# Two chunks of an input projection at a time by seven half products

## The chip, the cores and the metric

The kernel runs on one core of a Trainium2 chip: TensorE (PE) multiplies matrices, VectorE (DVE), ScalarE (ACT) and GpSimd (POOL) work elementwise, and SyncE (SP) issues most transfers. The metric is the device time of one execution in microseconds; less is better.

## The reference, cut to what matters

One inference step of a hybrid encoder with two layers. 512 prompt rows and 128 sample rows (8 sequences of 16) share all weights, so a layer works on 640 rows of 1024 features. A layer starts with one wide projection, whose columns feed four branches and their gates:

```python
(a_u, a_v, a_g, b_x, b_g, c_q, c_kv, c_kr, c_g, m_q, gate_logits) = split_cols(x @ w_in)
oa, v_rows = gmlp_branch(a_u, a_v, ...);      oa = oa * silu(a_g)
ob, conv_new, h_new = rglru_branch(b_x, ...); ob = ob * silu(b_g)
oc, ckv_new, kr_new = mla_branch(c_q, c_kv, c_kr, ...); oc = oc * silu(c_g)
om = mem_attend(m_q, mem_k, mem_v)
g = sigmoid(gate_logits)                      # 4 x 1024 columns
merged = g[0] * (oa @ w_br[A]) + g[1] * (ob @ w_br[B]) + g[2] * (oc @ w_br[C]) + g[3] * (om @ w_br[M])
x_new = layer_norm(ALPHA * x + merged @ w_out, ln_g, ln_b)
```

Everything is fp32. The branches are a chunked spatial gating (A), a short convolution with a linear recurrence (B), a latent attention (C) and an attention to a memory (M).

## The kernel before, in words

Every large product is done in three passes of a faster matmul type: a float32 matrix is split into a rounded part (`wh`, `xh`, type fp32r) and the rest (`wl`, `xl`), and `wh*xh + wh*xl + wl*xh` is accumulated in PSUM. `split` (L143 to L146) makes the two parts: a cast on ACT, a subtraction on DVE.

The activations are kept by features: `xh` and `xl` are two tiles each of 128 partitions x 4 x 640. Of the projection, 54 chunks of 128 columns per layer go through `fm_chunk`: it loads 128 x 1024 weights (`wload`, 512 KB), splits them, and calls `fm_product` (L112 to L126), which issues 8 x 3 steps of two matmuls of 320 columns each, 48 in all, into the two banks of one `acc` tile in PSUM (tag "acc", two tiles, four banks).

Chunks by use, per layer: 4 for `gelu_u` (u of A), 4 for the gate of C, 4 for the gate of A (`sga`), 2 for the memory's query (`mq`), 4 for the gate of B, 4 for the recurrence's input (`lru_in`), and 32 for the merge gates. `merge` is a generator: one step computes a gate chunk f of branch bi, its branch product y from `bhl` (the split branch result) and `w_br`, and adds the gated product to `macc` (on POOL for bi 1 and 2, on DVE in the last). In the last merge the sum is split again (`mgh`, `mgl`) for the output projection (L953).

The order of a layer in the program: latents and v, `gelu_u`, the queries (`q_ps`), the gate of C, keys and values, the latent attention of the sample (8 steps b: `ss_ps`, softmax `p_s`, transposes, `pt_s`, `olat_ps`), that of the prompt (4 blocks of 128 rows x 4 pairs of heads: `sc_ps`, maximum `mx`, exponential `p_c`, transposes `pt_ps`, copies `pt_c`, `pv_ps`), the gate of A, the mix of A (L623), the queries to the memory, the gate of B, the memory attention of the sample, then recurrence, memory attention of the prompt (`mem_prompt`) and first merge interleaved by hand, three more merges, output projection and normalisation.

The order on each engine is set at compile time by a list scheduler: an instruction is placed when its inputs are ready and its engine is free, earlier in the program first. Tiles live in pools; tiles of one tag share a number of slots. Those that matter here: tag "t" (five slots: `p_s`, `pt_s`, `olat`, `p_c`, `pt_c`, `p_m`, ...), tag "f" (two slots: `sga`, `mixb`, `g`, `a2`), "x" (four slots of 10 KB per partition) and "o" (four of 10 KB: `ep`, `v`, `oc`, `oa`, `um`, `ob`, `mgh`, `mgl`), "s" (one of 20 KB: `sc`, `wmx`, `bhl`, `wos`), "raw" (three of 4 KB) and "wh" and "wl" (two each, and two small ones).

The functions that the change touches, with their line numbers:

Of the kernel before, what the change touches and what calls it, by code (L numbers as in the profile page):

```python
# [9 lines left out]
F32 = mybir.dt.float32  # L10
# [30 lines left out]
def encoder_step(  # L41
# [19 lines left out]
    def xtile(name):  # L61
        return xp_.tile([128, 4, T], F32R, tag="x", name=name)
# [6 lines left out]

    def stile(shape, dtype, name):  # L70
        return big.tile(shape, dtype, tag="s", name=name)
# [31 lines left out]
    def wraw(src, n=1024):  # L103
        raw = wp.tile([128, n], F32, tag="raw", name="raw", bufs=3)
        nc.sync.dma_start(out=raw, in_=src)
        return raw

    def wload(src, n=1024):
        raw = wraw(src, n)
        sz = "" if n > 512 else "2"  # L110
        h = wp.tile([128, n], F32R, tag="wh" + sz, name="wh")
        lo = wp.tile([128, n], F32R, tag="wl" + sz, name="wl")  # L112
        split(h, lo, raw)
        return h, lo

# [12 lines left out]
    def tm_products(outs_, lhs_h, lhs_l, nc_, nk_per, width, load):  # L128
        for ci in range(nc_):
# [3 lines left out]
            for n, (j, a, w) in enumerate(steps):  # L133
                for t, o in enumerate(outs_):
# [3 lines left out]
                        rhs=w[:, j * width:(j + 1) * width],  # L138
# [36 lines left out]
    xscr = dr.tile([T, D], F32, name="xscr")  # L175

    for l in range(L):
# [12 lines left out]
        mh = kvtile([128, KD, 256], F32R, "mem_h")  # L190
        ml = kvtile([128, KD, 256], F32R, "mem_l")
        def mem_in(k):
            mt = wraw(ins["memT"][:, k:k + 4, :].rearrange("p a b -> p (a b)"))
            for m in range(2):
                split(
                    mh[:, k + 2 * m:k + 2 * m + 2, :], ml[:, k + 2 * m:k + 2 * m + 2, :],
                    mt[:, m * 512:(m + 1) * 512].rearrange("p (a b) -> p a b", a=2),
                )

        def w_mem(c):  # L200
            r = wload(ins["w_mem"][l, c])
# [42 lines left out]
        def w_c(c):  # L244
            if l > 0:
                return wload(ins["w_c"][l, c], 832)
            if c > 0:
                r = wload(ins["w_c"][l, c], 832)
                x_in(2 * c, 2)
                return r  # L250
            raw = wp.tile([128, 832], F32, tag="raw", name="raw", bufs=3)
            h = wp.tile([128, 832], F32R, tag="wh", name="wh")
            lo = wp.tile([128, 832], F32R, tag="wl", name="wl")
            for j in range(2):
                js = slice(416 * j, 416 * j + 416)
                nc.sync.dma_start(out=raw[:, js], in_=ins["w_c"][l, c][:, js])
                x_in(j, 1)
                split(h[:, js], lo[:, js], raw[:, js])
            return h, lo
# [7 lines left out]
        def fm_chunk(c, l=l):  # L267
            h, lo = wload(ins["w_fm"][l, c])
            o = acc("fm")
            fm_product(  # L270
                o,
                lambda k: h[:, k * 128:(k + 1) * 128],
                lambda k: lo[:, k * 128:(k + 1) * 128],
                xhk, xlk, KD,
            )
            return o[:, :, 0:TH]

# [29 lines left out]
        def w_v(c):  # L307
            r = wload(ins["w_v"][l, c])
# [799 lines left out]
```

## Time and profile before

| what | value |
|---|---|
| runs shown (3) | 1448.62 us median, 1448.54 to 1449.63 |
| profiled execution: span from first to last instruction | 1446.2 us |
| PE busy | 1426.0 us (99%), 9376 matmuls |
| DVE, ACT, POOL busy | 709.0 us (49%), 530.9 us (37%), 138.7 us (10%) |
| DMA | 134 MB, 28% of the 16 engines' time |

The time of the profiled execution itself is its span plus what lies around it, which the trace doesn't show; the median of the runs is 2.4 us above the span. A matmul's busy time overlaps that of the next, so its pace is read from the chain, not from its mean.

### The profile page before, as it was taken

How to read it: one execution, taken by the hardware profiler on the slowest of the kernel's cores; microseconds unless marked ns; L12 is line 12 of the kernel's file. 1: busy time of each engine (PE TensorE's matmuls, PEld its weight loads, DVE VectorE, ACT ScalarE, POOL GpSimd, SP SyncE). 2: the span in 40 equal slices, each digit the busy share in tenths (PEclk: the TensorE clock that was granted, in tenths of full speed). 3: DMA queues.
4: the chain of work that ended last, by engine and by line, in shares of the span. 5: the costliest groups of instructions: out<-in, count | busy, mean ns of one | idle time of the engine just before them, and what ended most of it. 6: DMA issues, size and time to landing. Idle time of an engine off the chain costs nothing.

```text
span 1446.2 us, 22712 instructions
## 1 busy us (share of the span) xinstructions
PE 1426.0 (99%) x9376; PEld 1322.8 (91%) x9376; DVE 709.0 (49%) x1264; ACT 530.9 (37%) x931; POOL 138.7 (10%) x200
## 2 busy tenths in 40 slices
PE   8999999999999999999999999999999999999997
PEld 8899888989999999998898998788899999999986
DVE  5643577386542232444834535763954322323546
ACT  5533443265532232333234434432664222222320
POOL 2020000010101112100111100000111011211000
PEclk9999999999999999999999999999999999999999
DMA  8342113213222222134372222032132222222323
GB/s 288 115 142 74 52 36 111 78 59 111 74 80 73 81 73 77 61 101 156 115 229 92 85 73 66 30 117 81 48 121 69 73 81 73 81 64 73 114 73 110
DMA packets 51065, 134.16 MB, mean 93 GB/s; under 512 B 5777, under 2 KB 14897, under 8 KB 49937
## 3 DMA queue, kind: packets, MB, share of 16 engines
q1 hardware_dynamic: 49328, 127.54, 27.7%
q0 software_dynamic: 1632, 5.16, 1.0%
q8 instruction: 74, 1.21, 0.4%
q14 instruction: 31, 0.25, 0.1%
HBM read 123.59 MB, written 7.78 MB: 91 GB/s over the span
## 4 chain that ended last, share of the span: by engine, by line
PE 93%; DVE 4%; ACT 1%; DMA 1%; issue 1%; DVEq 0%; POOL 0%; SPq 0%; ACTq 0%
PE fm L120 52%; PE y L120 14%; PE y_ps L953 6%; PE v L135 4%; PE c L135 3%; PE sc_ps L568 3%; PE pv_ps L592 2%; PE mem L135 2%; PE q_ps L120 1%; PE pt_ps L585 1%; PE gate L773 1%; PE mix L623 1%; PE ss_ps L513 1%; DVE wl L146 1%; PE ptm_ps L831 1%
## 5 line engine op out<-in xcount | busy, mean ns | idle before, releaser
L146 DVE TENSOR_TENSOR wl<-raw,wh 128x1024 fp32r<-128x1024 f32 (+4 forms) x203 | 206.0, 1016 | 419.4 <-issue 288.8
L120 PE MATMUL fm<-xh,wh 128*128 128x320 f32 x1728 | 406.9, 313 | 0.0
L120 PE MATMUL fm<-xl,wh 128*128 128x320 f32 x1728 | 404.1, 312 | 0.0
L145 ACT CAST wh<-raw 128x1024 fp32r<-128x1024 f32 (+4 forms) x203 | 179.2, 883 | 477.6 <-PE fm L120 326.8
L120 PEld LDWEIGHTS fm<-xh,wh 128*128 128x128 f32 x1728 | 289.3, 188 | 8.3 <-issue 5.0
L120 PEld LDWEIGHTS fm<-xl,wh 128*128 128x128 f32 x1728 | 289.6, 188 | 5.6 <-issue 4.9
L120 PE MATMUL fm<-xh,wl 128*128 128x320 f32 x1728 | 281.0, 311 | 0.0
L120 PEld LDWEIGHTS fm<-xh,wl 128*128 128x128 f32 x1728 | 258.7, 188 | 3.4 <-issue 2.6
L120 PE MATMUL y<-bhl,wh 128*128 128x320 f32 x896 | 141.6, 309 | 0.0
L120 PEld LDWEIGHTS y<-bhl,wh 128*128 128x128 f32 x896 | 133.6, 188 | 0.0
L884 POOL TENSOR_TENSOR macc<-macc,g 128x640 f32<-128x640 f32 x32 | 62.1, 1941 | 340.5 <-DVE g L881 340.5
L881 DVE SCALAR_TENSOR_TENSOR g<-g,y 128x640 f32<-128x640 f32 x48 | 39.4, 821 | 95.8 <-PE y L120 95.8
L120 PE MATMUL y<-bhl,wl 128*128 128x320 f32 x448 | 76.6, 309 | 0.0
L865 ACT ACTIVATE g<-fm 128x640 f32<-128x640 f32 x64 | 45.2, 706 | 81.4 <-PE fm L120 81.3
L120 PEld LDWEIGHTS y<-bhl,wl 128*128 128x128 f32 x448 | 68.3, 188 | 0.0
L568 PE MATMUL sc_ps<-kT,qT 128*128 128x128 f32 (+7 forms) x128 | 45.6, 450 | 0.0
L577 ACT ACTIVATE p_c<-sc_ps,mx 128x128 f32<-128x128 f32 (+3 forms) x64 | 33.6, 532 | 4.5 <-DVE mx L574 4.5
L953 PE MATMUL y_ps<-wo,mgh 128*128 128x512 f32 x120 | 35.1, 396 | 0.0
L587 ACT COPY pt_c<-pt_ps 128x128 f32<-128x128 f32 (+3 forms) x32 | 13.6, 425 | 52.8 <-PE pt_ps L585 52.8
L574 DVE TENSOR_REDUCE mx<-sc_ps 128x1 f32<-128x128 f32 (+3 forms) x64 | 30.3, 477 | 0.5
L585 PE MATMUL pt_ps<-ident,p_c 128*128 128x128 f32 x160 | 28.4, 275 | 1.7 <-DVE pt_c L587 1.7
L585 PEld LDWEIGHTS pt_ps<-ident,p_c 128*128 128x128 f32 x160 | 19.9, 140 | 10.8 <-issue 4.3
(295 smaller groups left out, 1675.2 us busy)
## 6 DMA issues: line engine op xcount, KB each, us to landing
raw<-in_w_fm SPq DMA_DIRECT2D x108, 512.0 KB, 3.5
raw<-in_w_br SPq DMA_DIRECT2D x48, 256.0 KB, 2.6
mcache<-in_mem_kv SPq DMA_DIRECT2D x8, 1024.0 KB, 4.8
raw<-in_w_out SPq DMA_DIRECT2D x16, 512.0 KB, 4.3
raw<-in_w_v SPq DMA_DIRECT2D x8, 512.0 KB, 4.0
raw<-in_w_mem SPq DMA_DIRECT2D x8, 512.0 KB, 3.5
raw<-in_w_c SPq DMA_DIRECT2D x7, 416.0 KB, 5.1
xr<-in_x SPq DMA_DIRECT2D x10, 256.0 KB, 3.0
```

Of the source, the lines that this page charges most:

```text
L120: PE.matmul(out=out[:, j, 0:TH], lhsT=a(k), rhs=b(k)[:, j * TH:(j + 1) * TH], start=(n == 0), stop=(n == len(steps) - 1),)
L135: PE.matmul(out=o[:, 0:width], lhsT=a(ci * nk_per + j)[:, t * 128:(t + 1) * 128], rhs=w[:, j * width:(j + 1) * width], start=(ci == 0 and ...
L145: ACT.copy(out=dst_h, in_=src)
L146: DVE.tensor_tensor(out=dst_l, in0=src, in1=dst_h.bitcast(F32), op=ALU.subtract)
L568: PE.matmul(out=s[:, 0:nk], lhsT=qT[0:kr_, h, ts_], rhs=kT[h // 4][0:kr_, h % 4, 0:nk], start=True, stop=True,)
L574: DVE.tensor_reduce(out=mx, in_=s[:, 0:nk], axis=AX.X, op=ALU.max, negate=True)
L577: ACT.activation(out=p[:, 0:nk], in_=s[:, 0:nk], func=AF.Exp, bias=mx, accum_out=sm)
L585: PE.transpose(tps[:, k * 128:(k + 1) * 128], p[:, k * 128:(k + 1) * 128], ident)
L865: ACT.activation(out=halves(g), in_=o, func=AF.Tanh, scale=0.5)
L881: DVE.scalar_tensor_tensor(out=halves(g), in0=halves(g), scalar=1.0, in1=y, op0=ALU.add, op1=ALU.mult)
L884: (POOL if bi < 3 else DVE).tensor_tensor(out=m, in0=m, in1=g, op=ALU.add)
L953: PE.matmul(out=o[j], lhsT=a[k // 4][:, k % 4, t * 128:(t + 1) * 128], rhs=w[:, j * 512:(j + 1) * 512], start=(k == 0 and p == 0), stop=(k ...
```

## The change

Two chunks c and c + 1 are computed together by `fm_pair`, with Strassen's scheme in Winograd's form: blocks are the two chunks, the two halves of the 1024 features and the two halves of the 640 rows. Seven products of half the depth and half the rows take the place of eight. Their weight operands are three blocks as loaded (a11, a12, a22) and four sums of blocks, made on POOL; their activation operands are blocks of x and four sums (`xt`), made once per layer by `x_sums`, one of them in place of a block of x. The seven results are combined by DVE from PSUM. 46 of the 54 chunks go this way, in 23 pairs per layer: gates of A and B, `mq`, `lru_in` and all merges. `gelu_u` and the gate of C stay as they were, since they come before `x_sums`.

```diff
-    xp_ = ctx.enter_context(tc.tile_pool(name="xpool", bufs=4))
-    op_ = ctx.enter_context(tc.tile_pool(name="opool", bufs=4))
+    op_ = ctx.enter_context(tc.tile_pool(name="opool", bufs=10))
...
+    def wraw(src, n=512):
+        raw = wtile("raw", n, "raw", 6)
+    def whl(raw, n=512):
+        h, lo = wtile("wh", n, "wh", 4), wtile("wl", n, "wl", 4)
+        split(h, lo, raw)
...
+    def spill(bi, k, src):
+        nc.sync.dma_start(out=oscr[bi][k], in_=src)
...
+        def x_sums():
+            for i in (2, 3, 4):
+                t_ = otile([128, 2, 4, TH], F32R, f"xt{i}")
+                xt[i] = t_[:, 0], t_[:, 1]
+            lo_, hi_ = slice(0, TH), slice(TH, T)
+            xt[11], xt[21] = ((xh[i][:, :, lo_], xl[i][:, :, lo_]) for i in range(2))
+            xt[22] = xh[1][:, :, hi_], xl[1][:, :, hi_]
+            xt[1] = xh[0][:, :, hi_], xl[0][:, :, hi_]
+            for k in range(4):
+                t12, t34, d = tmp([128, T], "t12"), tmp([128, T], "t34"), tmp([128, T], "td")
+                POOL.tensor_tensor(out=t3, in0=b12[0], in1=b22[0], op=ALU.subtract)
+                POOL.tensor_tensor(out=d[:, hi_], in0=b12[1], in1=b22[1], op=ALU.subtract)
+                POOL.tensor_tensor(out=t3, in0=t3, in1=d[:, hi_], op=ALU.add)
+                DVE.tensor_tensor(out=t1, in0=b11[0], in1=b12[0], op=ALU.subtract)
...
+                for i, t_ in ((2, t2), (3, t3), (1, t1), (4, t4)):
+                    split(xt[i][0][:, k, :], xt[i][1][:, k, :], t_)
+        def fm_pair(c, take):
+            a11, a12, a21, a22 = (
+                wraw(ins["w_fm"][l, c + e][:, i * 512:(i + 1) * 512]) for e in range(2) for i in range(2)
+            )
+            s1, s2, s3, s4 = (wtile("ws", 512, f"ws{i}", 4) for i in range(4))
+            for o, a, b in ((s1, a21, a22), (s2, a11, s1), (s3, a11, a21), (s4, a12, s2)):
+                POOL.tensor_tensor(out=o, in0=a, in1=b, op=ALU.add)
+            ab, cd = acc("fp"), acc("fp")
+            ba, bb, bc, bd = (o[:, j, 0:TH] for o in (ab, cd) for j in range(2))
+            def product(o, w, x, first, last):
+                h, lo = whl(w)
+                bh, bl = xt[x]
+                steps = [(k, h, b) for k in range(4) for b in (bh, bl)] + [(k, lo, bh) for k in range(4)]
+                for n, (k, a, b) in enumerate(steps):
+                    PE.matmul(out=o, lhsT=a[:, k * 128:(k + 1) * 128], rhs=b[:, k, :], ...)
+            z0, z1, t_ = ftmp([128, T], "z0"), ftmp([128, T], "z1"), tmp([128, T], "tu")
+            p1, u = t_[:, lo_], t_[:, hi_]
+            product(ba, a11, 11, True, False)
+            ACT.copy(out=p1, in_=ba)
+            product(bb, s2, 2, True, True)
+            DVE.tensor_tensor(out=u, in0=p1, in1=bb, op=ALU.subtract)
+            product(bc, s3, 3, True, False)
+            DVE.tensor_tensor(out=z1[:, hi_], in0=bc, in1=u, op=ALU.subtract)
+            product(bd, s1, 1, True, False)
+            DVE.tensor_tensor(out=z1[:, hi_], in0=z1[:, hi_], in1=bd, op=ALU.subtract)
+            product(ba, a12, 21, False, True)
+            take(0, lo_, ba)
+            product(bc, a22, 4, False, True)
+            DVE.tensor_tensor(out=z1[:, lo_], in0=bc, in1=u, op=ALU.subtract)
+            take(1, slice(0, T), z1)
+            product(bd, s4, 22, False, True)
+            DVE.tensor_tensor(out=z0[:, hi_], in0=bd, in1=u, op=ALU.add)
+            take(0, hi_, z0[:, hi_])
+            return z0, z1
...
         lru_in(0)
         lru_split(0)
         last = mem_prompt(0, last)
-        lru_in(1)
+        lru_gates(0)
         last = mem_prompt(1, last)
-        lru_gates(0)
         lru_rest(0)
+        lru_split(1)
         last = mem_prompt(2, last)
-        lru_in(2)
-        lru_split(1)
+        lru_gates(1)
         last = mem_prompt(3, last)
+        for c in range(2):
+            spill(3, c, om[:, c, :])
+        lru_rest(1)
         ma = merge(0)
         run_some(ma, 1)
-        lru_gates(1)
-        lru_rest(1)
+        lru_in(2)
         lru_split(2)
-        lru_in(3)
-        run_some(ma, 1)
         lru_gates(2)
```

What else changes with it:

- A pair is one step of `merge`: `fm_pair`, then two y products. `lru_in` handles two chunks per call.
- The branch results `oa`, `ob`, `oc`, `om` are written to DRAM (`spill`, on SP) when ready and read back into `osrc` (tag "t") at the start of their merge, after its first pair.
- Slots: x, `xt` and the branch tiles share tag "o" with ten slots; "s" is gone: `sc` is halved into `sc` and `scb`, `bhl` and `wos` are two tiles each. Weights are loaded, held and split in pieces of 512 columns: "raw" six slots, "wh" and "wl" four each, and four "ws" for the sums.
- `sga` moves from tag "f" to tag "t"; `z0` and `z1` of a pair take "f", `tu` takes "t".
- The mix of A moves from behind the prompt attention to behind `gelu_u`; `x_sums` stands between the attention of the sample and that of the prompt; the gate of B comes before the memory's query.

## Rows read from the trace of the kernel before

**Rows 1.** The page: busy time by engine, and the chain that ended last.
```profile
PE 1426.0 (99%) x9376; PEld 1322.8 (91%) x9376; DVE 709.0 (49%) x1264; ACT 530.9 (37%) x931; POOL 138.7 (10%) x200
...
PE 93%; DVE 4%; ACT 1%; DMA 1%; issue 1%; DVEq 0%; POOL 0%; SPq 0%; ACTq 0%
PE fm L120 52%; PE y L120 14%; PE y_ps L953 6%; PE v L135 4%; PE c L135 3%; PE sc_ps L568 3%; PE pv_ps L592 2%; PE mem L135 2%; PE q_ps L120 1%; PE pt_ps L585 1%; PE gate L773 1%; PE mix L623 1%; PE ss_ps L513 1%; DVE wl L146 1%; PE ptm_ps L831 1%
```

**Rows 2.** The chain in order of time: start us, us, what.
```profile
401.04 3.51 PE y L120 x24
404.55 7.04 PE fm L120 x48
...
1383.44 55.00 PE y_ps L953 x240
```

**Rows 3.** Windows of the fm matmuls on PE alone: length, busy (count), clock, DMA.
```profile
148.30:174.70 26.40, 13.62 (x65) 1.00 0.19 57
174.70:242.25 67.55, 31.83 (x146) 1.00 0.18 61
242.25:340.00 97.75, 71.54 (x451) 1.00 0.26 85
```

**Rows 4.** Windows: length, busy PE, PEld, DVE, ACT, POOL, clock, DMA share, GB/s.
```profile
148.30:174.70 26.40, 26.40 (x186) 21.14 (x184) 14.78 (x53) 10.79 (x32) 1.23 (x6) 1.00 0.19 57
174.70:242.25 67.55, 66.10 (x483) 52.38 (x482) 54.96 (x161) 30.47 (x86) 1.74 (x2) 1.00 0.18 61
...
300.00:325.00 25.00, 24.37 (x180) 21.15 (x180) 22.36 (x37) 18.54 (x42) 4.22 (x11) 1.00 0.15 49
...
400.00:600.00 200.00, 200.00 (x1367) 200.00 (x1366) 61.17 (x76) 51.00 (x67) 31.05 (x16) 1.00 0.23 72
...
1441.00:1446.00 5.00, 0.00 (x0) 0.00 (x0) 1.95 (x3) 0.00 (x0) 0.00 (x0) 0.58 0.28 105
```

**Rows 5.** Groups of instructions by form on DVE: busy us, mean ns, idle before.
```profile
L146 DVE TENSOR_TENSOR wl<-raw,wh 128x1024 fp32r<-128x1024 f32 x128 | 156.8, 1226 | 398.4 <-issue 288.8 <-PE fm L120 70.6 <-PE v L135 22.4
L881 DVE SCALAR_TENSOR_TENSOR g<-g,y 128x640 f32<-128x640 f32 x48 | 39.4, 821 | 95.8 <-PE y L120 95.8
L146 DVE TENSOR_TENSOR wl<-raw,wh 128x512 fp32r<-128x512 f32 x50 | 34.4, 688 | 3.3 <-ACT wh L145 3.3
L146 DVE TENSOR_TENSOR wl<-raw,wh 128x256 fp32r<-128x256 f32 x16 | 6.7, 417 | 0.0
```

**Rows 6.** Timeline of POOL in the second and third merge: two of its additions.
```profile
437.23 1.93 POOL L884 TENSOR_TENSOR macc<-macc,g 128x640 f32<-128x640 f32 x1 [40.97 <-DVE g L881]
...
584.97 1.67 POOL L884 TENSOR_TENSOR macc<-macc,g 128x640 f32<-128x640 f32 x1 [8.61 <-DVE g L881]
```

**Rows 7.** Timeline of DVE around these additions and around that at 511.10 us.
```profile
426.50 3.03 DVE L149 SCALAR_TENSOR_TENSOR bhl<-oc,bhl 128x640 fp32r<-128x640 f32 x4
...
437.06 0.68 DVE L146 TENSOR_TENSOR wl<-raw,wh 128x512 fp32r<-128x512 f32 x1
...
510.93 4.40 DVE L149 SCALAR_TENSOR_TENSOR bhl<-ob,bhl 128x640 fp32r<-128x640 f32 x4
...
584.80 0.42 DVE L146 TENSOR_TENSOR wl<-raw,wh 128x256 fp32r<-128x256 f32 x1
```

**Rows 8.** Transfers by line: count, KB each, median us to landing.
```profile
raw<-in_w_br SPq DMA_DIRECT2D x48, 256.0 KB, 2.6
```

**Rows 9.** Timeline of POOL: clearing `p_s` for the sample attention.
```profile
77.48 0.19 POOL L523 MEMSET p_s<- 128x128 f32 x1
...
112.69 0.21 POOL L523 MEMSET p_s<- 128x128 f32 x1 [1.26 <-DVE kT L468]
...
159.33 0.20 POOL L523 MEMSET p_s<- 128x128 f32 x1 [4.20 <-PE olat_ps L537]
```

**Rows 10.** Groups of DVE in the prompt attention, both layers.
```profile
L574 DVE TENSOR_REDUCE mx<-sc_ps 128x1 f32<-128x128 f32 (+3 forms) x64 | 30.3, 477 | 0.5
L579 DVE TENSOR_SCALAR p_c<-p_c,sm 128x128 f32<-128x128 f32 (+3 forms) x64 | 23.5, 372 | 0.6
```

More of the change, by code (lines that the diff above doesn't have):

```diff
@@ new lines, in fm_pair @@
+        def fm_pair(c, take):
+            a11, a12, a21, a22 = (
+                wraw(ins["w_fm"][l, c + e][:, i * 512:(i + 1) * 512]) for e in range(2) for i in range(2)
+            )
+            s1, s2, s3, s4 = (wtile("ws", 512, f"ws{i}", 4) for i in range(4))
[8 more added lines that the diff above has]
+                for n, (k, a, b) in enumerate(steps):
+                    PE.matmul(
+                        out=o, lhsT=a[:, k * 128:(k + 1) * 128], rhs=b[:, k, :],
+                        start=(first and n == 0), stop=(n == len(steps) - 1), skip_group_check=True,
+                    )
+            lo_, hi_ = slice(0, TH), slice(TH, T)
+            z0, z1, t_ = ftmp([128, T], "z0"), ftmp([128, T], "z1"), tmp([128, T], "tu")
[17 more added lines that the diff above has]
+            return z0, z1
@@ L474, in encoder_step @@
             for n, (a, b) in enumerate(((wh, ckh), (wl, ckh), (wh, ckl))):
-                PE.matmul(out=o, lhsT=a[:, ms], rhs=b, start=(n == 0), stop=(n == 2))
+                PE.matmul(out=o, lhsT=a[0][:, ms], rhs=b, start=(n == 0), stop=(n == 2))
             ACT.copy(out=kT[hp // 2][0:64, 2 * (hp % 2), :], in_=o[0:64, :])
@@ L482, in encoder_step @@
             for n, (a, b) in enumerate(((ckh, wh), (ckh, wl), (ckl, wh))):
-                PE.matmul(out=o, lhsT=a[:, ts_], rhs=b[:, 512:1024], start=(n == 0), stop=(n == 2))
+                PE.matmul(out=o, lhsT=a[:, ts_], rhs=b[1], start=(n == 0), stop=(n == 2))
             (DVE.tensor_copy if t % 2 else ACT.copy)(out=vc[:, t, :], in_=o)
@@ L555, in encoder_step @@
         )
+        x_sums()
         for i in range(4):
@@ new lines, in encoder_step, with silu_pair, take @@
+            spill(2, c, oc[:, c, :])
+        def silu_pair(c, dst):
+            def take(e, cols, z):
+                d = dst[e][:, cols]
+                ACT.activation(out=d, in_=z, func=AF.Tanh, scale=0.5)
+                DVE.scalar_tensor_tensor(out=d, in0=d, scalar=1.0, in1=z, op0=ALU.add, op1=ALU.mult)
+            fm_pair(c, take)
+        for c in (0, 2):
+            th = [tmp([128, T], f"sga{e}") for e in range(2)]
+            silu_pair(FM_AG + c, th)
+            for e in range(2):
+                DVE.tensor_tensor(out=oa[:, c + e, :], in0=oa[:, c + e, :], in1=th[e], op=ALU.mult)
+                spill(0, c + e, oa[:, c + e, :])
@@ L745, in lru_in @@
[L745 to L754 removed]
+            for e in range(2):
+                xp = lb[e][:, 0, :]
+                POOL.memset(xp[:, 0:3], 0.0)
+                POOL.tensor_copy(out=samp(xp)[:, :, 0:3], in_=cst[:, c + e, :, :])
@@ new lines, in take @@
+            def take(e, cols, z):
+                xp = lb[e][:, 0, :]
+                if cols.start == 0:
+                    ACT.copy(out=xp[:, 3:3 + TH], in_=z[:, 0:TH])
+                if cols.stop == T:
+                    z = z[:, z.shape[1] - TH:]
+                    ACT.copy(out=xp[:, 3 + TH:XP], in_=z[:, 0:n1])
+                    ACT.copy(out=samp(xp)[:, :, 3:XB], in_=z[:, n1:TH].rearrange("p (b t) -> p b t", b=NB))
+            fm_pair(FM_BX + c, take)
+            for e in range(2):
+                xp = lb[e][:, 0, :]
+                POOL.tensor_copy(out=lh[:, c + e, 9:12], in_=xp[:, XP - 3:XP])
+                POOL.tensor_copy(
+                    out=lh[:, c + e, 12:36].rearrange("p (b j) -> p b j", j=3), in_=samp(xp)[:, :, XB - 3:XB]
+                )
+                xc = lb[e][:, 1, 0:NXC]
+                DVE.tensor_scalar(
+                    out=xc, in0=xp[:, 0:NXC], scalar1=conv_w[:, c + e, 0:1], scalar2=conv_b[:, c + e:c + e + 1],
+                    op0=ALU.mult, op1=ALU.add,
+                )
+                for k in range(1, 4):
+                    DVE.scalar_tensor_tensor(
+                        out=xc, in0=xp[:, k:k + NXC], scalar=conv_w[:, c + e, k:k + 1], in1=xc,
+                        op0=ALU.mult, op1=ALU.add,
+                    )
```

284 lines of the change are left out of this document (140 added, 144 removed).

## The prediction

> **What bounds the kernel now.** I read the page first: TensorE is busy 99% of the span, and the chain that ended last runs through PE for 93% of it, 52% in the matmuls of `fm_chunk` alone [rows 1]. A busy PE isn't yet PE at its pace, so I read the chain in order of time in the merge: a chunk's 48 matmuls take 7.04 us, 146.7 ns each, the y product behind it 24 in 3.51 us, the same, with nothing between [rows 2]. So wherever PE is fed, a removed matmul is worth 146.7 ns. The table by stretches says where that is: in 400 to 600 us PE is never idle and VectorE works 61 of 200 us [rows 4]. The attention stretches are another matter: 148 to 175 us (sample) and 175 to 242 us (prompt) keep PE busy too, but VectorE works 55 of 67.6 us in the second, and PE stays busy because chunks fill its waits: 65 fm matmuls in the first stretch, 146 in the second [rows 3, 4]. The whole question is whether the new form still can fill there.
>
> **What is removed.** A pair was 2 x 48 matmuls and is 7 x 12 = 84 of the same shape. 23 pairs a layer, two layers, 12 each: 552 matmuls x 146.7 ns = **80.9 us**. That twelve matmuls in a row now go into one bank costs nothing: the output projection's 240, whose last group does that, run at an even 229 ns [rows 2]. LDWEIGHTS goes with its matmul, one each, as before.
>
> **What a pair adds.** VectorE: the lo parts were two subtractions of 1024 columns, 2 x 1.23 us, and are seven of 512, 7 x 0.69; five sums of 320 columns lie between 0.42 (256) and 0.69 (512), I take 0.49 [rows 5]. That is 4.8 + 2.4 - 2.5 = 4.8 us more per pair. GpSimd: four sums of 512. Its own time for a two-input add has to be read out of the waits: the add of 640 columns takes 1.93 us where VectorE had begun a two-input subtraction 0.17 us before, which ends 0.51 us after the add's start, and 1.67 us where the subtraction ends after 0.25 us [rows 6, 7]. Both leave 1.42 us: the two engines take turns. The other way round, four two-input operations of VectorE take 4.40 us with one such add among them against 3.03 without [rows 7]. So 512 columns cost 1.42 x 512/640 = 1.14 us of turn (1.93 x 512/640 = 1.54 with the wait), a pair 4.6 to 6.2 us.
>
> In the first three merges a step is PE 12.3 + 7.0 = 19.3 us, VectorE 9 x 0.69 + 2.4 + 2 x 0.82 = 10.3, GpSimd 4.6 + 2 x 1.42 = 7.4; even laid end to end these stay under it: **nothing**. In the last merge y is half as long: PE 15.8, VectorE 7 x 0.69 + 2 x 0.42 + 2.4 + 6 x 0.82 = 13.0, GpSimd 4.6, end to end 17.6. Bounds 0 to 4 x 1.8 = 7 us per layer; I take 1, as most of GpSimd's adds can fall beside VectorE's reads of PSUM.
>
> A rule speaks against giving GpSimd these sums. The Trainium skill, "GPSIMD Engine Reference", Performance versus the Vector engine, calls it the wrong engine for ordinary two-input arithmetic, about twice as slow, 4497 ns for 2048 columns; by that, an estimate, 512 cost 1.12 us and a pair 4.5. The rows put it between 4.6 and 6.2 us. On VectorE the four would be 2.75 us on the engine that the last merge already fills, so here the rule would not shorten the sum.
>
> Hidden: the w_fm loads halve to 256 KB, the size of w_br's, which land in 2.6 us [rows 8], with up to six in flight and casts four products (7 us) ahead of PE. The branch results go out and come back under whole pairs of 12.3 us, on DMA engines that are 0.2 busy [rows 4]; the read-back is queued on SP behind weight loads, and without cover it would cost a landing, some 3 us, per merge. The mix moves forward with its matmuls and costs PE the same there, as fm chunks beside it hide its waits.
>
> **What fills no longer.** Slots of a tag are handed out in the order in which the program first touches its tiles. The row for this: `p_s` of the sample attention is cleared at 77.48 and 112.69 us, long before use, each time as soon as one slot came free (`krt`'s last reader at 112), and the fifth at 159.33, right after the `olat` matmuls had released a `pt_s` [rows 9]. Later tiles don't overtake. In the new order of tag "t": the twelve temporaries of `x_sums` stand between the sample's last and the prompt's first, and the pair's `tu` and `sga` stand behind the prompt attention's last. A pair can issue products 1 to 4 early, but product 5 needs bank `ba` after `p1`, and `p1` lives in `tu`. So per layer:
>
> (1) Sample attention. 65 fm matmuls, 9.5 us, were its fill [rows 3]; now product 1 alone, 1.8 us. The stretch shortens by what the fill delayed it, so 0 to 7.8 us of idle; I take 6, since its chain of small steps on three engines didn't wait for the fill at most steps.
>
> (2) `x_sums`. Per k: three GpSimd operations of 320 columns, 2.1 us, and eleven on VectorE (seven sums, four splits), all with both inputs in SBUF, so they take turns: 11 x 0.40 = 4.4 us at the least (back to back, a quarter of 3.03 for 640 columns, halved [rows 7]) to 11 x 0.49 + 2.1 = 7.5. With five slots the prompt's first exponential comes after three of four k: 13 to 22 us. Off that go up to 4 us of start while the sample attention ends, and 5 us in which PE has products 2 to 4. 4 to 17 us; I take 10.
>
> (3) Prompt attention. 146 fm matmuls were its fill, 21.4 us, and the mix [rows 3]; now what is left of 36. Without them it needs PE some 40 us (66.1 less 21.4 and less the mix's 4.5) and VectorE 43 (half of `mx`'s 30.3 and of `p_c`'s 23.5 [rows 10], the rest copies, memsets and reciprocals), less some 2 us of fill: idle is 1 us if VectorE alone sets the end, 13 if the stretch lasts 55. I take 7.
>
> (4) Memory attention and recurrence. VectorE is at 22.4 of 25 us in 300 to 325 us now [rows 4], with 451 fm matmuls to fill over 242 to 340 [rows 3]. Three pairs bring 14 us more to it, and `lru_in(2)` now stands directly before `lru_gates(2)`: sums, copies, four convolution steps and a cast, about 5 us in which the next pair waits behind the gates for its banks. 4 to 19 us; I take 10.
>
> (5) The last merge, 1.
>
> Sum per layer 6 + 10 + 7 + 10 + 1 = 34 (bounds 9 to 64), both layers 68. Against 80.9: **-13 us**. The profiled execution spans 1446.2; the median of the runs is 2.4 us above it (what lies around the span). 1446.2 - 13 + 2.4 = **1435.6, I say 1435**.
>
> **Rivals.**
> (A) Slower: the idle of (2) decides. If sums and splits take strict turns, the gap is 17 us and the prompt attention behind it starts with VectorE still in the last k, 14 in place of 7: 6 + 17 + 14 + 10 + 1 = 48 per layer, 1448.6 - 80.9 + 96 = 1464. It decides from 42 us per layer. For it: the turns [rows 6, 7]; against: PE reads parts of VectorE's results as they come.
> (B) The fill is found after all: if the gap is near its lower bound and the recurrence hides under gates and pairs, 17 per layer, 1448.6 - 80.9 + 34 = 1402. For it: PE is idle 1.5 us in all of 175 to 242 now, so the order is a good one; against: that order had chunks to place.
> (C) The clock. It is granted at 1.00 (2.4 GHz) in every stretch here, and at 0.58 only in the last 5 us, in which PE does nothing [rows 4]. A gap like (2) could let it fall to 1.2 GHz. No row has matmuls at that level, so the price lies between nothing and twice the time for what PE does in and right behind the gaps of (1) and (2), the 48 early products, 7 us per layer: up to 14 us in all, 1435 + 14 = 1449, no change. The Trainium skill, "TensorE: Matmul & The Clock Gate", Part 1, says that an idle PE goes back to 1.2 GHz; no run here shows it between matmuls.
>
> **Chances.** Likeliest, 28 to 38 us per layer (1424 to 1444): 0.41. (B) and all below 28 (down to 1386): 0.20. (A) and all above 42: 0.24; (C) with more than its 14 us, also slower: 0.06; within 0.2% (3 us, about what a measurement of this kernel tells from no change): 0.09, most of it (C). Faster 0.61, same 0.09, slower 0.30. Range 1393 to 1474: from well into (B) to beyond (A), one in ten left out on each side.
>
> **What would show it.** PE's count falls by 552 to about 8,824; merge steps of 19.3 us where two of 10.55 stood; in each layer a stretch after the sample attention with PE little busy and VectorE and GpSimd alternating on `xt`; products 5 of the first pair only after the last `pv_ps`. Wrong if pair products appear throughout the prompt attention (then B), if PE idles inside the merges (then the turns cost more than laid out), or if an fm-shaped matmul isn't 147 ns any more.

## The result, and the profile after

The changed kernel takes 1649.99 us (median of 4 runs, 1648.43 to 1661.99) against 1448.8: the ratio is 1.140, with a 95% interval of 1.137 to 1.144. It is 201 us slower; I had forecast 1435, and nothing above 1474 in my range.

The page of the changed kernel, the lines that answer to [rows 1]:

```profile
PE 1455.1 (88%) x8824; PEld 1287.6 (78%) x8824; DVE 1079.4 (66%) x1879; ACT 676.7 (41%) x1340; POOL 439.5 (27%) x408
...
PEclk9999579987999999999999995799879999999999
...
PE 69%; DVE 16%; issue 5%; ACT 4%; POOL 3%; DMA 3%; SPq 1%; DVEq 0%; POOLq 0%; ACTq 0%
PE fp L327 26%; PE y L123 10%; PE y_ps L1074 7%; PE fm L123 6%; DVE wl L149 4%; PE v L138 3%; PE c L138 3%; PE sc_ps L677 3%; POOL ws L318 2%; PE pt_ps L694 2%; PE pv_ps L701 2%; PE mem L138 1%; DMA raw<-in_w_fm 1%; DVE lb L853 1%; PE gate L875 1%
```

The 552 matmuls are gone, yet PE is busy 29 us longer and idle 192 us (20 before): the chain holds PE for 69% where it held it for 93%, and in two places per layer the clock falls. Where, the windows show. First the kernel before, layer 0, cut at the sample attention's first and last matmul, the prompt attention's first and last `pv_ps`, the last `gate` and the last y (columns as in [rows 4]):

```profile
148.30:174.80 26.50, 26.50 (x187) 21.23 (x185) 14.78 (x53) 10.79 (x32) 1.23 (x6) 1.00 0.20 59
174.80:177.36 2.56, 2.56 (x18) 2.30 (x18) 0.98 (x2) 1.39 (x3) 1.09 (x1) 1.00 0.37 131
177.36:242.25 64.89, 63.44 (x466) 50.00 (x465) 53.98 (x159) 29.09 (x84) 0.65 (x1) 1.00 0.17 58
242.25:383.45 141.20, 139.56 (x1025) 128.76 (x1026) 77.60 (x116) 68.00 (x124) 11.71 (x31) 1.00 0.27 87
383.45:664.86 281.41, 281.41 (x1921) 281.41 (x1921) 101.10 (x139) 82.30 (x107) 34.16 (x22) 1.00 0.26 81
```

The changed kernel at the same marks (the fourth stretch is cut once more, at the first `mss_ps` of the memory attention):

```profile
152.46:179.21 26.75, 22.70 (x124) 15.52 (x122) 12.99 (x46) 9.04 (x28) 5.64 (x12) 0.83 0.06 21
179.21:203.35 24.14, 7.78 (x20) 4.53 (x19) 24.09 (x52) 8.26 (x22) 8.57 (x9) 0.50 0.00 0
203.35:268.79 65.44, 52.11 (x295) 30.73 (x295) 40.35 (x135) 22.57 (x76) 0.00 (x0) 0.81 0.11 37
268.79:338.26 69.47, 65.14 (x418) 61.13 (x418) 54.58 (x79) 30.33 (x55) 27.20 (x18) 1.00 0.36 118
338.26:478.90 140.64, 107.62 (x697) 91.78 (x698) 90.44 (x143) 68.50 (x138) 32.37 (x47) 0.85 0.22 70
478.90:764.49 285.59, 269.76 (x1758) 259.38 (x1758) 198.22 (x281) 119.98 (x207) 114.62 (x74) 0.99 0.30 98
```

The matmuls of pairs alone on PE in the same kernel, which answers to [rows 3]: in the gap 12, in the whole prompt attention one.

```profile
152.46:179.21 26.75, 1.56 (x7) 0.83 0.06 21
179.21:203.35 24.14, 6.12 (x12) 0.50 0.00 0
203.35:268.79 65.44, 0.07 (x1) 0.81 0.11 37
268.79:338.26 69.47, 65.14 (x417) 1.00 0.36 118
338.26:478.90 140.64, 55.51 (x317) 0.85 0.22 70
478.90:764.49 285.59, 185.68 (x1176) 0.99 0.30 98
```

From these, each stretch's loss in layer 0: its length, less what it took before, corrected by 0.1467 us for each chunk or pair matmul more or fewer (the same view of `fm` before counts 66, 15, 132, 646 and 1344; the y are as many) and by 5.4 us for the mix that left the prompt attention.

| stretch | before | after | matmuls moved | lost | forecast |
|---|---|---|---|---|---|
| (1) sample attention | 26.5 | 26.8 | -59 | 9 | 6 |
| (2) gap of `x_sums` | 2.6 | 24.1 | -3 | 22 | 10 |
| (3) prompt attention | 64.9 | 65.4 | -131, mix | 25 | 7 |
| (4) memory, recurrence | 141.2 | 210.1 | +88 | 56 | 10 |
| (5) merges from the last gate on | 281.4 | 285.6 | -168 | 29 | 1 |

The sum is 141 us; less the 40 us of removed matmuls and some 3 us gained at the layer's two ends that makes the 98 us by which layer 0 is longer (724 before, 822 after). Layer 1 repeats it. The experiments take these five apart, (4) only in part.

### The profile page after: what moved, and what is told of

It reads as the page before. It is cut to its first block, busy times and chain, and to the rows that moved or that the text cites. A ratio compares the mean times of both kernels' runs of the same rounds, so it can differ in the third digit from the quotient of the medians.

```text
span 1646.7 us, 24079 instructions
## 1 busy us (share of the span) xinstructions
PE 1455.1 (88%) x8824; PEld 1287.6 (78%) x8824; DVE 1079.4 (66%) x1879; ACT 676.7 (41%) x1340; POOL 439.5 (27%) x408
## 4 chain that ended last, share of the span: by engine, by line
PE 69%; DVE 16%; issue 5%; ACT 4%; POOL 3%; DMA 3%; SPq 1%; DVEq 0%; POOLq 0%; ACTq 0%
PE fp L327 26%; PE y L123 10%; PE y_ps L1074 7%; PE fm L123 6%; DVE wl L149 4%; PE v L138 3%; PE c L138 3%; PE sc_ps L677 3%; POOL ws L318 2%; PE pt_ps L694 2%; PE pv_ps L701 2%; PE mem L138 1%; DMA raw<-in_w_fm 1%; DVE lb L853 1%; PE gate L875 1%
## 5 line engine op out<-in xcount | busy, mean ns | idle before, releaser
L149 DVE TENSOR_TENSOR wl<-raw,wh 128x512 fp32r<-128x512 f32 (+2 forms) x292 | 279.5, 967 | 130.5 <-ACT wh L148 64.8
L148 ACT CAST wh<-raw 128x512 fp32r<-128x512 f32 (+2 forms) x292 | 175.9, 604 | 326.6 <-PE fp L327 196.3
L327 PE MATMUL fp<-xh,wh 128*128 128x320 f32 x736 | 227.7, 326 | 42.3 <-DVE z L346 25.5
L327 PE MATMUL fp<-xt,wh 128*128 128x320 f32 x1104 | 206.9, 326 | 39.6 <-ACT xt L148 17.4
L327 PE MATMUL fp<-xl,wh 128*128 128x320 f32 x736 | 220.6, 311 | 0.0
L327 PEld LDWEIGHTS fp<-xt,wh 128*128 128x128 f32 x1104 | 172.9, 195 | 60.2 <-ACT xt L148 19.6
L318 POOL TENSOR_TENSOR ws<-raw,ws 128x512 f32<-128x512 f32 x92 | 140.0, 1521 | 215.3 <-DVE wl L149 155.1
L327 PEld LDWEIGHTS fp<-xh,wh 128*128 128x128 f32 x736 | 139.4, 189 | 61.9 <-DVE z L346 29.6
L149 DVE TENSOR_TENSOR wl<-ws,wh 128x512 fp32r<-128x512 f32 x184 | 138.8, 755 | 4.8 <-ACT wh L148 3.7
L327 PEld LDWEIGHTS fp<-xl,wh 128*128 128x128 f32 x736 | 139.6, 190 | 0.6 <-issue 0.4
```

The source lines that it names most:

```text
L148: ACT.copy(out=dst_h, in_=src)
L149: DVE.tensor_tensor(out=dst_l, in0=src, in1=dst_h.bitcast(F32), op=ALU.subtract)
L318: POOL.tensor_tensor(out=o, in0=a, in1=b, op=ALU.add)
L327: PE.matmul(out=o, lhsT=a[:, k * 128:(k + 1) * 128], rhs=b[:, k, :], start=(first and n == 0), stop=(n == len(steps) - 1), skip_group_chec ...
```

## The experiments

Times below are single runs beside the kernel before on the same chip (1448 to 1451), unless a ratio is given. 1650 is the changed kernel; its own four runs lie up to 14 us apart, so a single run nearer to it than that shows nothing by its time alone.

**no_pairs**: all but the pairs. Merges and the other 14 chunks go through `fm_chunk`, with the recurrence's order of before.

```diff
-        x_sums()
...
-                z = fm_pair(22 + br * 8 + f, take)
+                z = [ftmp([128, T], "g") for e in range(2)]
+                for e in range(2): ACT.activation(out=halves(z[e]), in_=fm_chunk(22 + br * 8 + f + e), ...)
```

> No chunk goes in pairs and x_sums is gone; what stays of the change is all else: pieces of 512 columns, ten slots of tag o, branch results through DRAM, the mix ahead, merge steps of two chunks. If the loss is that of the pairs, as I think: 1445 to 1465 (9376 matmuls, PE near 97% busy). If slots, queues or the trips through DRAM make a good part of it: over 1480.

1449.1 us. Slots, halved loads, the trips through DRAM and the mix moved ahead cost nothing; the whole loss is that of the pairs and `x_sums`.

**x_sums_out, sums_out, gate_a_direct, merge_only.**

```diff
x_sums_out, in place of x_sums' loops:
+            xt[2], xt[3], xt[4] = xt[11], xt[22], xt[21]
sums_out, in place of the four POOL sums:
+            s1, s2, s3, s4 = a21, a11, a21, a12
gate_a_direct:
-            silu_pair(FM_AG + c, th)
+            silu_into(th, FM_AG + c)      # for c in range(4), th = ftmp(...)
merge_only: so for the gate of B, mq and lru_in too
```

> x_sums is left out (the pairs multiply blocks of x in place of its sums; 7 products, casts and combinations as they were). Theory 'fill' (idle that nothing can fill: the gap behind the sample attention is the work of x_sums itself): the gap of 24 us per layer goes, the prompt attention stays near 65 us at full clock or less; 1650 - 2 x 22 = about 1606. Theory 'clock' (the gap lets the clock fall and the prompt attention behind it pays): the prompt attention also falls from 65 to under 55 us, 1570 to 1590. Theory 'turns' (VectorE and GpSimd block each other in the pairs and this makes the loss): 1640 to 1650, since the pairs' own sums stay.

> The four sums of weight blocks on GpSimd are left out (the products take raw blocks in their place; as many casts, subtractions, products and combinations as before). Theory 'turns': the subtractions fall from a mean of 0.97 to 0.69 us, the merges lose their 24 us of idle per layer, the recurrence some 15 of its 56: 1650 - 2 x 39 = about 1572. Theory 'banks' (a product waits until VectorE has read the other bank of the same PSUM tile, whatever GpSimd does): the merges keep 15 or more of the 24 us, 1625 to 1650. Theory 'fill': the stretch from the end of the prompt attention to the last gate stays over 190 us (210 now).

> The gate of A goes back to four direct chunks with its temporary in tag f, in the same place of the program; all else as in the changed kernel. It has 12 matmuls more per pair, 2 x 2 x 12 x 0.147 = 7 us in all. Theory 'fill': the 4 chunks (28 us of matmuls) run inside the sample attention, the gap and the prompt attention, where PE is idle 54 us per layer now; the two pairs' 26 us behind the prompt attention go, and the clock stays at 1.00 there, worth 5 to 15 us more: 1650 - 2 x (26 to 41) = 1568 to 1598. Theory 'turns': no fill is missing, 1650 or some us more.

> All chunks ahead of the merges are direct again (gates of A and B, memory query, recurrence input, with the hand order of the kernel before); only the 16 pairs of merge gates per layer stay, with x_sums where it is. Theory 'fill': the losses ahead of the merges (110 us per layer by the trace) go; 32 pairs x 12 x 0.1467 = 56 us are saved and the merges' 2 x 24 us of idle stay, x_sums adds 5 to 15 us of VectorE per layer to stretches that it nearly fills: 1449 - 56 + 48 + 2 x (5 to 15) = 1451 to 1471. Theory 'clock' or 'x_sums': its gap stays open although chunks could fill it, 2 x 22 more: about 1500.

x_sums_out: 1595.0, between what 'fill' and 'clock' said. The gap shrinks from 24.1 to 2.5 us, the prompt attention only from 65.4 to 63.4. sums_out: 1602.4; the subtractions of 512 columns fall from a mean of 906 ns (260 of raw blocks at 1013, 184 of sums at 755) to 723, and the rest of the merges from 285.6 to 269.1. gate_a_direct: 1613.0, between what the two theories said, and merge_only 1540.2, where 1451 to 1500 was expected. Much of the reason is in `x_sums`: it writes one of its sums over a block of x (`xt[1]` is a part of `xh[0]`, `xl[0]`). A direct chunk that stands behind it in the program must wait for it (and computes with the overwritten block, in these two runs as in rec_direct below). So in gate_a_direct no chunk matmul runs in the sample attention and the gap stays 28 us; 139 run in the prompt attention, which at a clock of 1.00 is 66.6 us long.

**banks, sums_dve, mq_first, warm_gap.**

```diff
banks:
-            ba, bb, bc, bd = (o[:, j, 0:TH] for o in (ab, cd) for j in range(2))
+            X, Y = tiles if turn[0] else tiles[::-1]; turn[0] = not turn[0]
+            ba, bc, bb, bd = (o[:, j, 0:TH] for o in (X, Y) for j in range(2))
...          # product(bd, s4, 22, ...) and its readers now ahead of product(bc, a22, 4, ...)
-                    y = acc("y")
+                    y = [bank_s("y0"), bank_s("y1")] if e == 0 else [bank_t("y0"), bank_o("y1")]
sums_dve:
-                POOL.tensor_tensor(out=o, in0=a, in1=b, op=ALU.add)
+                DVE.tensor_tensor(out=o, in0=a, in1=b, op=ALU.add)
mq_first: the lines of um and fm_pair(FM_MQ, ...) ahead of those of ob
warm_gap, behind each split of x_sums (and 10 per step b of the sample attention):
+                    for n in range(9):
+                        PE.matmul(out=dm[:, n % 2, 0:TH], lhsT=xh[0][:, k, 0:128], rhs=xt[i][0][:, k, :], ...)
```

> The pair's results lie in PSUM so that no product is followed by one into the other bank of the same tile (ba with bc, bb with bd, the seventh product ahead of the sixth, the two tiles change roles from pair to pair), and y takes the four banks that stand idle in the merges. Same operations, but the y gating in two halves. Theory 'banks' (a product waits until VectorE has read the other bank of its tile, about 1 us at the sixth and seventh product): the back-to-back pairs fall from 13.3 to under 12.7 us, the merges lose 8 to 15 of their 24 us of idle: 1650 - 2 x (11 to 18) = 1614 to 1628. Theory 'turns' alone: the operands' low parts are late, wherever results lie: 1640 to 1655.

> The four sums of weight blocks move from GpSimd to VectorE. With them left out, the merges gained 16.5 us per layer and the whole 46 us. Theory 'turns': on VectorE they cost 4 x 0.69 = 2.8 us per pair there but no subtraction is slowed (0.97 back to 0.69, 7 x 0.28 = 2.0 us): VectorE about as full as now, the idle of PE behind a blocked subtraction goes, 1605 to 1630. Rival 'in order': VectorE's queue, on which the results of the products are read too, gets longer and later, 1650 to 1680.

> The memory's query is computed ahead of the gate of B, as in the kernel before; all else unchanged. Theory 'fill' (from the first mss_ps to the last gate PE has too few pairs to run beside the attention to the memory, 140 us with 810 us-equivalents of 0.147 us matmuls, before 103): two more pairs run beside the memory attention, PE's 48 us of idle there falls by 10 to 20 us per layer: 1610 to 1630. Theory 'late weights' (the weights of the next pair are queued behind other transfers and their sums come late): nothing changes in that, 1640 to 1655. Theory 'recurrence' (two chunks share both buffers lb, so the chain of the four chunks runs one behind the other): the idle moves from the memory attention to the recurrence, 1640 to 1655.

> Matmuls of 320 columns whose result nobody reads are put into the sample attention (10 per step, into unused columns of its score bank) and into x_sums (9 behind each of its 16 splits), so that PE is busy there. Nothing is left out. Theory 'clock': the granted clock stays at 1.00 through the gap and the prompt attention falls from 65 to under 58 us, 1650 - 2 x (8 to 15) = 1620 to 1634. Theory 'chain' (the length of the prompt attention is that of its chain of scores, maximum, exponential, transposes and copies, with or without fill: 64.9 us before, 63 to 67 here in every run): it stays at 62 to 66 us with the clock at 1.00, 1640 to 1655.

banks: 1572.0, 78 us less, far more than I had expected. sums_dve: 1605.0, as much as leaving the sums out. mq_first: 1648.9; the query is there at 315 us, but `qbd` is written only at 331 (337.6 in the changed kernel) and the first `mss_ps` stays at 338. Only 34 more pair matmuls run from there to the last gate, in 143.6 and 142.2 us (140.6 and 142.6), so the run says little of 'fill'. The 810 in its expectation doesn't fit the trace: in the 140.6 us PE ran 697 matmuls, 413 of them of pairs and y. warm_gap: 1655.7 in all, since the added matmuls lengthen the sample attention and the gap to 32 and 30 us; but the prompt attention falls to 58.2 us at a clock of 1.00, in both layers.

**rec_direct, lru_w_slot, late_pairs.**

```diff
rec_direct: lru_in(c), its fm_chunk and the order of calls as in the kernel before
lru_w_slot:
-            raw = wraw(ins["lru_w"][l, c], 256)
+            raw = wp.tile([128, 256], F32, tag="lraw", name="raw", bufs=1)     # and "raw" with 5 slots
late_pairs: merge_only and banks, and
-            for i in (2, 3, 4):
+            for i in (1, 2, 3, 4):                      # xt[1] gets a tile of its own
+                if bi == 0: z = ...                     # first merge by fm_chunk, as in no_pairs
...
         nc.gpsimd.dma_start(out=outs["lh"][l], in_=lh)
+        x_sums()                                        # no longer ahead of the prompt attention
         run_some(ma, 9)
```

> Only the four chunks of the recurrence's input are direct again, in the hand order of the kernel before, so that chunk c writes lb[c % 2] by itself; they read a block of x that x_sums has overwritten. 4 x 12 = 48 matmuls more (2 x 24 x 0.147 = 7 us in all). Theory 'recurrence' (a pair fills both buffers lb, so that the four chains of convolution, gates and scan run one behind the other, with PE waiting): first mss_ps to last gate falls from 141 to 115 to 125 us: 1650 - 2 x (15 to 25) = 1600 to 1620. Theory 'late weights': it stays over 135, 1640 to 1655.

> The recurrence's weights (lru_w) are loaded into a tile of their own, not into one of the slots of tag raw, of which five are left (six before). Theory 'late weights' (lru_w's raw tile waits up to 18 us for its single lwl, and every later load on SP's queue waits behind it, so that weights land when PE already stands): first mss_ps to last gate falls by 8 to 20 us per layer, 1650 - 2 x (8 to 20) = 1610 to 1634. Theory 'recurrence': no change, or slower by the lost slot: 1645 to 1665.

> Pairs only in the merges 2 to 4 (12 per layer), with results and y in the banks as in the run banks; everything ahead, the first merge too, is direct; x_sums stands behind the recurrence, beside the direct steps of the first merge, and writes a fourth tile of its own in place of a block of x. Nothing is left out. Theory: where PE is fed and no product waits for the other bank, a pair is worth its 12 x 0.1467 = 1.76 us: 24 pairs, 42 us; x_sums hides under the first merge, where VectorE works a third of the time; 1449 - 42 + (0 to 16) = 1407 to 1423. Rival: VectorE and GpSimd (x_sums, sums) or the late fourth tile of mg hold PE in the merges all the same, 1430 to 1460.

rec_direct: 1610.0. From the first `mss_ps` to the last gate it takes 137.3 us, more than I had expected, but with 573 chunk, pair and y matmuls in it where 413 ran in 140.6: 160 x 0.1467 = 23 us more work in 3 us less. lru_w_slot: 1655.7; the stretch falls to 134.1 and 137.5 us (140.6 and 142.6), less than expected, and the two attentions ahead of it give that back (33 us for the sample where it was 27). That needn't be the lost slot's doing: the granted clock is 0.59 there, 0.83 in the changed kernel, and kernels with six slots show the same (below, under (1)). late_pairs: 1430.2, below the kernel before, but above the 1407 to 1423 of its theory and at the lower edge of its rival.

**pair_banks, y_banks, banks_sums_out, late_pairs_2.** The two halves of banks; banks with the four sums left out; and `x_sums()` moved behind `run_some(ma, 9)`.

```diff
late_pairs_2:
-        x_sums()
         run_some(ma, 9)
+        x_sums()
```

> The half of the run banks that concerns the pair: places of the results, order of the last two products, roles of the two tiles; y stays in the tiles that the pairs use. Theory 'inside the pair' (the sixth and seventh product wait for readers of the other bank): most of the 78 us that banks gained, 1575 to 1600; back-to-back pairs as in banks, 66 us for five. Theory 'between pair and y' (y and the next pair wait for each other's readers in the same two tiles): the merges keep over half of their 24 us per layer, 1600 to 1640.

> The other half of the run banks: y in the four banks that stand idle in the merges, the pair as in the changed kernel. Theory 'inside the pair': little, 1630 to 1650, and the five pairs ahead of the memory attention stay at 69 to 71 us. Theory 'between pair and y': 1590 to 1620.

> The run banks without the four sums of weight blocks (raw blocks in their place, as in sums_out). If VectorE and GpSimd taking turns cost PE time only because a product waits for VectorE to read the other bank, the merges stay at 260 to 262 us per layer, and the gain over banks (1572) is under half of the 46 us that sums_out gained: 1550 to 1572. If turns and banks are two separate losses, the gains add: about 1526.

> As late_pairs (1430), with x_sums one step later in the program, behind the last step of the first merge, so that VectorE gives the recurrence and the first merge priority: from the first mss_ps to the last gate late_pairs took 131.4 us, no_pairs 125.6. Theory 'x_sums delays the recurrence': these 6 us per layer come back, 1418 to 1426. Rival: x_sums then ends too late for the second merge's first pairs, which wait for it: 1428 to 1445.

pair_banks 1592.5; y_banks 1648.3; banks_sums_out 1560.8, with raw blocks in place of the sums. late_pairs_2: 1428.46 (1427.73 to 1429.78) against 1449.03, ratio 0.986 with an interval of 0.984 to 0.988: 1.4% faster than the kernel before, the best version here, and in the rival's range. By its count it should be 288 x 0.1467 = 42 us faster and is 21. From the first `mss_ps` to the last gate it takes 130.1 and 131.4 us, late_pairs 131.4, no_pairs 125.6. But the edit moved nothing: the scheduler begins `x_sums` at the same place in both kernels. Timeline of DVE, its first operation in late_pairs (61 us behind the first `mss_ps`):

```profile
341.42 1.17 DVE L302 TENSOR_TENSOR td<-xl 128x320 f32<-128x320 f32 x1
```

And in late_pairs_2 (61 us too):

```profile
340.35 1.17 DVE L302 TENSOR_TENSOR td<-xl 128x320 f32<-128x320 f32 x1
```

So its theory is untested. The stretch in no_pairs and in late_pairs_2 (columns as in [rows 4]) shows VectorE 16 us and GpSimd 15 us busier, with as many chunk and y matmuls, which speaks for `x_sums`; no run takes it out there, so that stays open.

```profile
280.34:405.94 125.60, 122.79 (x911) 112.06 (x911) 78.67 (x126) 70.11 (x137) 10.52 (x31) 1.00 0.35 112
279.51:409.60 130.09, 124.33 (x910) 113.32 (x909) 94.60 (x160) 68.80 (x140) 25.71 (x43) 0.99 0.27 90
```

Windows of the rest of the merges in layer 0, from the last gate to the last y, 1752 pair and y matmuls in all. In sums_out:

```profile
470.47:739.61 269.14, 266.00 (x1758) 257.74 (x1758) 164.80 (x281) 121.02 (x207) 33.19 (x22) 1.00 0.32 103
```

In y_banks:

```profile
487.28:770.15 282.87, 268.53 (x1754) 258.81 (x1754) 199.43 (x307) 120.22 (x207) 115.01 (x74) 0.99 0.30 98
```

In pair_banks:

```profile
469.68:733.87 264.19, 260.72 (x1754) 258.50 (x1753) 187.42 (x281) 118.58 (x208) 114.69 (x74) 0.99 0.33 105
```

In banks:

```profile
467.38:729.36 261.98, 258.88 (x1753) 257.21 (x1754) 189.34 (x308) 118.38 (x207) 114.73 (x74) 1.00 0.33 105
```

In banks_sums_out:

```profile
460.61:718.39 257.78, 257.78 (x1754) 257.21 (x1754) 165.26 (x307) 118.65 (x207) 34.11 (x22) 1.00 0.33 105
```

Against 285.6 in the changed kernel: with the banks as they were, the sums cost 16.5 us; with the banks apart, 4.2. The pair's half of the edit alone brings 21.4, y's half 2.7. VectorE is as full in banks (189 of 262 us) as in the changed kernel (198 of 286), so it was not its load by itself that held PE.

## Why the prediction was wrong

**The removed matmuls** were right: 8,824 are left, and twelve in a row into one bank keep the pace. In banks_sums_out 1752 take 257.8 us, 147.1 ns each.

**(5), the step that failed most plainly: "even laid end to end these stay under it: nothing".** I added up each engine's work per step and did not ask which result a product waits for. A merge step of the changed kernel in its chain in order of time, which answers to [rows 2]:

```profile
630.45 9.19 PE fp L327 x60
...
639.67 1.78 DVE wl L149 x2
641.45 0.83 issue
642.29 0.49 DVE z L346
642.82 2.03 PE fp L327 x12
644.85 6.31 PE y L123 x43
```

From 639.64 to 642.82 us the chain isn't PE's. PE itself issues the sixth product and five matmuls of y in that time, then stands. Timeline of PE, the seventh product's first matmul:

```profile
642.82 0.41 PE L327 MATMUL fp<-xh,wh 128*128 128x320 f32 x1 [0.71 <-DVE z L346]
```

PE's waits in these merges say the same (us in total, times, longest):

```profile
PE fp L327 <- DVE z L346: 7.0, 9, 1.3
PE fp L327 <- DVE z L995: 3.8, 2, 2.9
PE fp L327 <- DVE z L342: 2.6, 4, 0.9
```

L346 reads bank `bc` after the sixth product; the seventh writes `bd`, another bank, but of the same tile, and the program lets it wait for all readers of the tile. No other product of the pair lies between the two. VectorE comes to L346 late because its queue has two subtractions ahead, which take turns with GpSimd's sums. Timeline of POOL one step on:

```profile
659.47 1.29 POOL L318 TENSOR_TENSOR ws<-raw 128x512 f32<-128x512 f32 x1 [5.42 <-ACT wh L148]
660.84 1.62 POOL L318 TENSOR_TENSOR ws<-raw,ws 128x512 f32<-128x512 f32 x1
662.42 1.73 POOL L318 TENSOR_TENSOR ws<-raw 128x512 f32<-128x512 f32 x1
```

And of DVE:

```profile
659.74 3.27 DVE L149 TENSOR_TENSOR wl<-raw,wh 128x512 fp32r<-128x512 f32 x2
662.94 0.48 DVE L346 TENSOR_TENSOR z<-fp,tu 128x320 f32<-128x320 f32 x1
```

Two subtractions take 3.27 us for 2 x 0.69 [rows 5]. The sums' own price I had right at its upper end, 1.14 to 1.54 us; the groups of POOL by form:

```profile
L318 POOL TENSOR_TENSOR ws<-raw,ws 128x512 f32<-128x512 f32 x92 | 140.0, 1521 | 215.3 <-DVE wl L149 155.1 <-issue 56.0 <-POOL lb L829 0.9
L318 POOL TENSOR_TENSOR ws<-raw 128x512 f32<-128x512 f32 x92 | 138.7, 1508 | 356.9 <-DMA raw<-in_w_fm 264.8 <-ACT wh L148 38.2 <-DVE wl L149 34.6
```

What I left out is the other side of the turns. The groups of DVE by form: over the kernel the subtraction of a raw block takes 1013 ns, that of a sum 755.

```profile
L149 DVE TENSOR_TENSOR wl<-raw,wh 128x512 fp32r<-128x512 f32 x260 | 260.9, 1013 | 114.8 <-ACT wh L148 54.5 <-PE fm L123 32.1 <-PE v L138 17.1
L149 DVE TENSOR_TENSOR wl<-ws,wh 128x512 fp32r<-128x512 f32 x184 | 138.8, 755 | 4.8 <-ACT wh L148 3.7 <-PE fm L123 1.0
```

In sums_out:

```profile
L149 DVE TENSOR_TENSOR wl<-raw,wh 128x512 fp32r<-128x512 f32 x444 | 318.3, 723 | 121.2 <-ACT wh L148 46.6 <-PE fm L123 37.6 <-PE v L138 17.1
```

The merge rows above show how the two join. The changed kernel is 27.8 us over banks_sums_out; without the sums 11.4 of these are left, with the banks apart 4.2. The two gains overlap: most of what the sums cost, they cost through the shared tile. The Trainium skill, "PSUM — Partial Sum Buffer", Summary: rules for kernel authors, says to read a bank other than the one that is written and to guard by bank with semaphores; here the guard was by tile of two banks. No run guards by bank; with the results placed and ordered so that one product lies between a read and the next write to the same tile (pair_banks), the stretch is 21.4 us shorter. And the page of the Trainium skill that I had weighed and set aside, "GPSIMD Engine Reference", Performance versus the Vector engine, was the better counsel: I wrote that the four sums on VectorE "would not shorten the sum"; they shortened the run by 45 us.

**(3): "idle is 1 us if VectorE alone sets the end, 13 if the stretch lasts 55".** I priced the lost fill as if the prompt attention would shrink to one engine's own work or little more. It doesn't. Windows of three kernels. no_pairs, with 143 chunk matmuls in it:

```profile
180.94:241.93 60.99, 60.99 (x438) 46.63 (x437) 47.67 (x146) 27.58 (x84) 0.60 (x1) 1.00 0.23 78
```

warm_gap, without chunks, with 20 pair matmuls, at full clock:

```profile
214.53:272.72 58.19, 46.03 (x316) 28.53 (x315) 40.91 (x136) 23.64 (x78) 0.00 (x0) 1.00 0.14 46
```

x_sums_out, without either, at a lower clock:

```profile
183.07:246.49 63.42, 50.03 (x295) 29.58 (x295) 40.15 (x134) 22.61 (x76) 0.00 (x0) 0.85 0.10 34
```

143 matmuls, 21 us of work, cost no more than a few us there (61.0 against 58.2, which holds 20 pair matmuls itself): they were all but free, and taking them out gave almost nothing back. No engine is full in 58.2 us (PE 46, VectorE 41), so I take it that the chain of small steps sets the length, which I had read as VectorE's sum; no view shows that chain by itself. Of the 25 us lost in (3), some 18 are this, and 7 the clock.

**(1), 9 for 6.** Here the step held: I had taken most of the lost fill as idle, and the sample attention takes 26.8 us without fill, 26.5 with it. What lies above my bound of 7.8 I put down to the clock, granted at 0.83 there. The same 124 matmuls in the two layers of sums_dve:

```profile
152.83:179.62 26.79, 22.78 (x124) 15.52 (x122) 13.45 (x47) 9.09 (x28) 4.28 (x10) 0.82 0.06 21
946.76:980.12 33.36, 30.51 (x124) 20.06 (x122) 12.79 (x47) 9.04 (x28) 4.29 (x10) 0.57 0.05 16
```

Both layers of the changed kernel's profiled run were of the first kind (26.8 us at 0.83), by luck: at the second's clock (1) would have lost some 7 us more per layer.

**(2), 22 for 10.** VectorE is busy 24.09 of 24.14 us in the gap, and x_sums_out removes it. Its price per k was right: 26.4 us for the 44 operations, 6.6 per k, where I had 4.4 to 7.5. The first exponential came where I had it, at 197.41 us, 18 into the gap; but VectorE then works off the last k among the first block's steps, and the first `pv_ps` comes only at 203.35. And only 3 of the 44 operations, 1.5 us, began while the sample attention ended, where I had allowed up to 4 us. And of the 36 matmuls of products 2 to 4 that I had let cover 5 us of the gap, 12 ran there. So the loss lies beyond my upper bound of 17. That the slots of tag "t" keep pairs out of the prompt attention was right: one pair matmul in it. I overlooked that the sum written over a block of x bars direct chunks too.

**(4), 56 for 10.** At least three causes, whose shares overlap. The recurrence: rec_direct gives back 40 us in all, 7 more matmul time included, some 23 per layer. A pair delivers two chunks at once, into both buffers `lb`, and VectorE runs both convolutions, eight operations where I had counted four, before the first chunk's cast. Timeline of DVE in the changed kernel, the first and the last of the eight:

```profile
367.42 0.63 DVE L848 TENSOR_SCALAR lb<-lb,vec 128x664 f32<-128x664 f32 x1 [0.29 <-ACT lb L834]
...
374.38 0.90 DVE L853 SCALAR_TENSOR_TENSOR lb<-lb,vec 128x664 f32<-128x664 f32 x1
```

And of PE, which stands 5 us for the first gates behind that cast:

```profile
376.11 0.92 PE L875 MATMUL gate<-lx,lwh 128*128 128x332 f32 x2 [5.12 <-ACT lx L148]
```

Banks and sums: the stretch falls from 210 to 188 us when both are out of the way (banks_sums_out), 22 per layer. If these two didn't overlap, about 11 would be left for late weights, missing fill and the clock, which mq_first and lru_w_slot did not separate. The clock was granted at 0.85 from the first `mss_ps` on, and no run with these pairs held it at 1.00 there.

**The rivals.** (A) had the right sign and named the gap, but at 1464 it held 15 of the 201 us. (C), the clock, was no rival but one more cost: 0.50 granted in the gap and 0.81 in the prompt attention, which takes 65.4 us in layer 0 and 67.4 in layer 1 where warm_gap takes 58.2: 7 to 9 us per layer, near the 7 that I had as its bound, but by luck: I had priced the 48 early products alone and not the attention's own matmuls. The sample attention and the second half of (4), where the clock fell too, come on top of that. The Trainium skill, "TensorE: Matmul & The Clock Gate", Part 1, says that an idle PE goes back to 1.2 GHz. I could only cite it; now the trace agrees: PE was busy 7.8 of 24.1 us in the gap, and the clock granted was 0.50, the 1.2 GHz level.

## What to carry to other kernels

Work that fills another stage's waits costs that stage next to nothing, so removing it from there gains nothing; save operations where the engine is fed (late_pairs_2 keeps 24 of the 46 pairs, all in the merges, and is 1.4% faster). When an engine's results are read by another, look at the tile that the next instruction writes, not only at its bank: order and place results so that one product lies between a read and the next write to the same tile. A sum of each engine's work per step bounds nothing as long as it does not say who waits for whom.

## What the runs showed of the hardware

That VectorE's subtractions and GpSimd's additions in SBUF slow each other was in [rows 6, 7]; how much it is over a kernel was not expected: a mean of 906 ns where 688 stood, and 723 with the sums gone. And a run of matmuls that nobody reads (warm_gap) kept the granted clock at 1.00 and 0.95 through the sample attention of the two layers and brought the prompt attention from 65.4 and 67.4 to 58.2 us, though the kernel as a whole got no faster.
